# Banded attention: scores from float32r halves of q and k, three products in place of one fp32 product

## The chip, the cores and the metric

The kernel runs as one program on 1 core of one Trainium2 chip. The metric is the device time of that core in microseconds (us), from runs of the whole program. TensorE is called PE, its weight loads PEld, VectorE DVE, ScalarE ACT, GpSimd POOL and the SyncE queue SP. One execution was taken with the hardware profiler; its rows are what the texts below read.

## The reference, cut to what matters

The model is a trunk of two layers over 256 positions of width 2048. The first layer mixes by retention, the second by a sliding-window attention; each layer then has a SwiGLU block and a gated embedding. The change touches the attention mixer alone:

```python
proj = h @ w_in
q, k, v = jnp.split(proj, [SWA_Q_WIDTH, SWA_Q_WIDTH + SWA_KV_WIDTH], axis=-1)
q = (q * (HD ** -0.5)).reshape(B, NB, W, HKV, G, HD)      # 2 blocks of 128, 4 kv heads, 8 heads each, 64 wide
...
s = jnp.einsum('bqkgd,bskd->bkgqs', qb, kb).astype(jnp.float32) + alibi
s = jnp.where(valid, s, -jnp.inf)
m = jnp.maximum(jnp.max(s, axis=-1, keepdims=True), sink)
e = jnp.exp(s - m)
probs = e / (jnp.sum(e, axis=-1, keepdims=True) + jnp.exp(sink - m))
return jnp.einsum('bkgqs,bskd->bqkgd', probs.astype(vb.dtype), vb)
```

There are 32 query heads in 4 groups of 8; each group shares one k and one v. A query block of 128 sees its own block and the one before it, so the first block has 128 keys and the second 256.

## The kernel before, in words

All large products are made in float32r from two halves. A weight unit (128 x 2 x 512, 512 KB) is loaded on SP, ACT copies it to a float32r tile `hi` (L211), DVE subtracts to get `lo` (L212), and `multiply` issues, for each of 2 k-tiles and 2 row tiles, three products: high by high (L161), high by low (L162), low by high (L163). One unit is 12 products of 512 columns on PE; units are loaded 5 ahead and split 3 ahead.

The work between the large products is held in generators on the list `side`. After each unit, `step_side` runs every generator to its next `yield`. So the source gives an order in which small pieces of attention stand between units. The scheduler of the framework then lays out each engine's queue from that, with its own estimates, and may move small pieces past each other; each engine works through its queue in that fixed order and waits on semaphores of the others.

In the attention stage `kv_done` scales k and v; its `later` transposes k on PE into a PSUM tile `tr` (2 buffers, `transpose_pair`, L224) and copies it into `kT` with DVE (L436). For each of the 4 kv heads, `q_done` scales eight heads of q, and its `later` transposes them (8 transposes, two `tr` tiles) and copies one `tr` with DVE (L527) and the other with ACT (L525) into `qT`. Then come four calls of `scores(i)`, two heads each: 64 rows of the PE array hold one head (e = 0), the other 64 the second (e = 1). Per head there are two plain fp32 products (L460), of 128 columns for block 0 and of 256 for block 1, into two PSUM tiles `at` (2 buffers). DVE adds the bias (L470), takes the maximum (L479) and makes the exponents' offset `nm` (L488); ACT makes the exponentials with row sums (L493) and those of the sinks (L496); `normalise` adds (L500), inverts (L502) and scales (L506, four per call); `transpose_probs` transposes them on PE (L512) into `tr`, and DVE (L516) and ACT (L514) copy them into `pT`. The products with v are L544, and their result is split (L211, L212) into `oT`, which feeds the output projection.

The helper at the centre of the change is the split, which for an unscaled source is an ACT copy followed by a DVE subtraction that reads the ACT result:

```python
nc.scalar.activation(hi, src, AF.Copy)
nc.vector.tensor_tensor(lo, src, hi.bitcast(F32), op=ALU.subtract)
```

Of the kernel before, what the change touches and what calls it, by code (L numbers as in the profile page):

```python
# [11 lines left out]
F32 = mybir.dt.float32  # L12
F32R = mybir.dt.float32r
# [5 lines left out]
P = 128  # L19
D = 2048  # L20
S = 256
# [8 lines left out]
SH, SD, SKV = 32, 64, 4  # L30
# [57 lines left out]
def tile_trunk(ctx, tc, ins, out):  # L88
    nc = tc.nc
# [313 lines left out]
    def swa(norm, next_norm, w_in, w_out):  # L403
        ol = Lhs()
        st = {}
# [10 lines left out]

        def kv_done(acc):
            sp = stage.pool
            kT = st["kT"] = sp.tile([P, SKV, S], F32, name="kT")
            v = st["v"] = sp.tile([P, NT, SKV * SD], F32, name="vs")  # L420
            kd = sp.tile([P, NT, SKV, 2, SD], F32, name="kd")
            inv8 = st["inv8"] = sp.tile([P, NT], F32, name="inv8")
            nc.vector.tensor_scalar_mul(inv8, norm.inv, SD**-0.5)
            for t in range(NT):
                src = acc[t][:, 0 : SKV * SD].rearrange("p (j d) -> p j d", d=SD)
                for e in range(2):
                    nc.scalar.activation(kd[:, t, :, e, :], src, AF.Copy, scale=norm.inv[:, t : t + 1])
                nc.scalar.activation(
                    v[:, t, :], acc[t][:, SKV * SD : 2 * SKV * SD], AF.Copy, scale=norm.inv[:, t : t + 1]
                )  # L430

            def later():
                for i in range(2):
                    yield
                    tr = transpose_pair(blocks(lambda t: kd[:, t].rearrange("p j e d -> p (j e d)"), i))
                    nc.vector.tensor_copy(kT[:, 2 * i : 2 * i + 2, :], tr)  # L436

            return later()

        def q_done_of(j):  # L440
            def q_done(acc):
                sp, kT, v, rel = stage.pool, st["kT"], st["v"], st["rel"]
                q = sp.tile([P, NT, NW], F32, name="q")
                for t in range(NT):
                    nc.scalar.activation(q[:, t, :], acc[t], AF.Copy, scale=st["inv8"][:, t : t + 1])
                qT = sp.tile([P, 4, S], F32, name="qT")
                sc = sp.tile([P, GH, 3, P], F32, name="sc")
                pT = sp.tile([P, 3, 2, 4, P], F32, name="pT")

                def block(h, b):  # L450
                    blk = sc[:, h, 0:1, :] if b == 0 else sc[:, h, 1:3, :]
                    return blk.rearrange("p a b -> p (a b)")

                def scores(i):

                    ats = [ps_at.tile([P, 3 * P], F32, name="at") for _ in range(2)]
                    for b in range(2):
                        for e in range(2):
                            sl = slice(e * SD, (e + 1) * SD)
                            nc.tensor.matmul(  # L460
                                ats[e][:, 0:P] if b == 0 else ats[e][:, P : 3 * P],
                                qT[sl, i, b * P : (b + 1) * P],
                                kT[sl, j, 0 : (b + 1) * P],
                                start=True,
                                stop=True,
                            )
                    hs = slice(2 * i, 2 * i + 2)
                    for e in range(2):
                        h = 2 * i + e
                        nc.vector.scalar_tensor_tensor(  # L470
                            out=sc[:, h].rearrange("p a b -> p (a b)"),
                            in0=rel,
                            scalar=-(2.0 ** (-8.0 * (j * GH + h + 1.0) / SH)),
                            in1=ats[e],
                            op0=ALU.mult,
                            op1=ALU.add,
                        )
                    mx = small.tile([P, 2, 3], F32, name="mx")
                    nc.vector.reduce_max(mx, sc[:, hs], axis=AX.X)  # L479
                    sk = st["sink"][:, j * GH + 2 * i : j * GH + 2 * i + 2]  # L480
                    nc.vector.tensor_tensor(mx[:, :, 1], mx[:, :, 1], mx[:, :, 2], op=ALU.max)
                    mm = small.tile([P, 2, 2], F32, name="mm")
                    es = small.tile([P, 2, 2], F32, name="es")
                    for b in range(2):
                        nc.vector.tensor_tensor(mm[:, b, :], mx[:, :, b], sk, op=ALU.max)
                        nc.vector.tensor_tensor(es[:, b, :], sk, mm[:, b, :], op=ALU.subtract)
                    nm = small.tile([P, 2, 2], F32, name="nm")
                    nc.vector.tensor_scalar_mul(nm, mm, -1.0)  # L488
                    den = small.tile([P, 2, 2], F32, name="den")
                    for e in range(2):  # L490
                        for b in range(2):
                            blk = block(2 * i + e, b)
                            nc.scalar.activation(  # L493
                                blk, blk, AF.Exp, bias=nm[:, b, e : e + 1], accum_out=den[:, b, e : e + 1]
                            )
                    nc.scalar.activation(es, es, AF.Exp)  # L496
                    return den, es

                def normalise(i, den, es):
                    nc.vector.tensor_tensor(den, den, es, op=ALU.add)  # L500
                    rd = small.tile([P, 2, 2], F32, name="rd")
                    nc.vector.reciprocal(rd, den)  # L502
                    for e in range(2):
                        for b in range(2):
                            blk = block(2 * i + e, b)
                            nc.vector.tensor_scalar_mul(blk, blk, rd[:, b, e : e + 1])  # L506

                def transpose_probs(i):
                    for e in range(2):
                        tr = ps_tr.tile([P, 3, P], F32, name="tr")  # L510
                        for b in range(3):
                            nc.tensor.transpose(tr[:, b, :], sc[:, 2 * i + e, b, :], ident)  # L512
                        if e:
                            nc.scalar.copy(pT[:, :, e, i, :], tr)  # L514
                        else:
                            nc.vector.tensor_copy(pT[:, :, e, i, :], tr)  # L516

                def later():

                    yield  # L520
                    yield
                    for i in range(2):
                        tr = transpose_pair(blocks(lambda t: q[:, t, :], i))
                        if i:
                            nc.scalar.copy(qT[:, 2 * i : 2 * i + 2, :], tr)  # L525
                        else:
                            nc.vector.tensor_copy(qT[:, 2 * i : 2 * i + 2, :], tr)  # L527
                    for i in range(4):
                        yield
                        part = scores(i)  # L530
                        if i > 1:
                            transpose_probs(i - 2)
                        yield
                        normalise(i, *part)
                    yield
                    transpose_probs(2)
                    yield
                    transpose_probs(3)
                    yield
                    for b in range(2):  # L540
                        o = ps_at.tile([P, 4, P], F32, name="at")
                        for e in range(2):
                            for m in range(b + 1):
                                nc.tensor.matmul(  # L544
                                    o[e * SD : (e + 1) * SD, :, :],
                                    v[:, m, j * SD : (j + 1) * SD],
                                    pT[:, 0 if b == 0 else 1 + m, e, :, :],
                                    start=m == 0,
                                    stop=m == b,
                                )  # L550
                        ks, sl = slice(4 * j, 4 * j + 4), slice(b * P, (b + 1) * P)
                        split(ol.hi[:, ks, sl], ol.lo[:, ks, sl], o)
                    ol.ready.update(range(4 * j, 4 * j + 4))

                return later()

            return q_done
# [5 lines left out]
        n = KD // KU  # L563
# [303 lines left out]
```

## Time and profile before

| | us |
|---|---|
| median of 3 runs (2621.5 to 2621.99) | 2621.93 |
| the profiled execution, its own time | 2622.02 |
| its span, first to last instruction | 2619.9 |
| PE busy in the span | 2607.7 |
| DVE busy | 1814.4 |
| ACT busy | 1223.2 |

The attention's score products lie between about 1602 and 1722 us of the span. A matmul's own duration is longer than the distance to the next, since matmuls overlap in the array; what a stretch costs on PE is read from the distances between starts. In the timeline one plain fp32 product is two records, one float32r product is one; equal instructions that follow each other are merged into one row with their count.

### The profile page before, as it was taken

Reading aid. Unit: us, or ns where it says so; the run is one execution under the profiler, and the core shown is the slowest. Engines: PE = TensorE matmul, PEld = TensorE weight load, DVE = VectorE, ACT = ScalarE, POOL = GpSimd, SP = SyncE. Lnnn points to the kernel's source line nnn. Section 1 sums busy time; section 2 is a strip of 40 time slices with the busy share of each in tenths; the row PEclk is TensorE's granted clock in tenths of the full one; section 3 lists DMA queues with packets and bytes.
Section 4 is the critical chain, followed back from the end, with each engine's and each line's share of the span. In section 5 each row is a group of like instructions: output and inputs, shape, how many; then the busy total and the mean of one; then the engine's idle time right before and its main releaser. Section 6 shows DMA issues by size and latency. Waiting matters only on the chain.

```text
span 2619.9 us, 31288 instructions
## 1 busy us (share of the span) xinstructions
PE 2607.7 (100%) x11641; PEld 2144.0 (82%) x11641; DVE 1814.4 (69%) x2563; ACT 1223.2 (47%) x1531; POOL 15.1 (1%) x31
## 2 busy tenths in 40 slices
PE   9999999999999999999999999999999999999998
PEld 7888888888888888888888888777888888888887
DVE  7777777766666666666555786888757575755565
ACT  6444444444444444444444555555444444444444
POOL 0000000000000000000000000000000000000000
PEclk9999999999999999999999999999999999999999
DMA  8556555566666666666666665346665666666664
GB/s 288 187 186 188 184 188 179 185 186 191 196 194 198 189 199 189 197 191 195 193 194 193 191 196 169 123 144 199 190 198 189 198 189 198 190 196 193 193 209 144
DMA packets 139481, 497.79 MB, mean 190 GB/s; under 512 B 15808, under 2 KB 16960, under 8 KB 139200
## 3 DMA queue, kind: packets, MB, share of 16 engines
q1 hardware_dynamic: 139040, 495.73, 60.5%
q8 instruction: 91, 1.49, 0.2%
q14 instruction: 62, 0.51, 0.1%
q10 hardware_dynamic: 288, 0.07, 0.0%
HBM read 493.63 MB, written 2.10 MB: 189 GB/s over the span
## 4 chain that ended last, share of the span: by engine, by line
PE 94%; DVE 3%; DMA 1%; issue 1%; ACT 0%; POOL 0%; ACTq 0%; POOLq 0%; SPq 0%; DVEq 0%
PE acc L161 31%; PE acc L163 30%; PE acc L162 30%; DVE xt L236 1%; DVE lo L212 1%; PE at L460 1%; DMA x<-in_xT 1%; PE tr L512 0%; DMA xs<-in_x 0%; PE at L544 0%; PE at L329 0%; DVE xTl L215 0%; DMA pt<-in_pT 0%; PE at L356 0%; PE at L358 0%
## 5 line engine op out<-in xcount | busy, mean ns | idle before, releaser
L212 DVE TENSOR_TENSOR lo<-raw,hi 128x1024 fp32r<-128x1024 f32 (+1 forms) x929 | 1131.3, 1221 | 701.2 <-ACT hi L211 693.7
L211 ACT ACTIVATE hi<-raw 128x1024 fp32r<-128x1024 f32 (+1 forms) x929 | 980.8, 1058 | 1186.8 <-PE acc L163 1074.9
L161 PE MATMUL acc<-hi,xTh 128*128 128x512 f32 x2592 | 1009.5, 390 | 0.7 <-ACT hi L211 0.5
L163 PE MATMUL acc<-hi,xTl 128*128 128x512 f32 x2592 | 1008.1, 389 | 1.2 <-DVE xTl L215 1.2
L162 PE MATMUL acc<-lo,xTh 128*128 128x512 f32 x2592 | 1008.1, 389 | 0.0
L161 PEld LDWEIGHTS acc<-hi,xTh 128*128 128x128 f32 x2592 | 487.1, 188 | 104.4 <-issue 3.0
L163 PEld LDWEIGHTS acc<-hi,xTl 128*128 128x128 f32 x2592 | 487.0, 188 | 103.8 <-DVE xTl L215 2.1
L162 PEld LDWEIGHTS acc<-lo,xTh 128*128 128x128 f32 x2592 | 487.1, 188 | 100.9 <-DVE lo L212 0.8
L161 PE MATMUL acc<-hi,hTh 128*128 128x512 f32 x704 | 273.9, 389 | 0.0
L162 PE MATMUL acc<-lo,hTh 128*128 128x512 f32 x704 | 273.9, 389 | 0.0
L163 PE MATMUL acc<-hi,hTl 128*128 128x512 f32 x704 | 273.9, 389 | 0.0
L236 DVE STREAM_TRANSPOSE xt<-h 32x256 f32<-32x256 f32 x352 | 153.4, 436 | 6.8
L161 PEld LDWEIGHTS acc<-hi,hTh 128*128 128x128 f32 x704 | 132.2, 188 | 27.7
L162 PEld LDWEIGHTS acc<-lo,hTh 128*128 128x128 f32 x704 | 132.2, 188 | 27.4
L163 PEld LDWEIGHTS acc<-hi,hTl 128*128 128x128 f32 x704 | 132.2, 188 | 27.2
L236 DVE STREAM_TRANSPOSE xt<-xs 32x256 f32<-32x256 f32 x320 | 139.5, 436 | 6.0
L161 PE MATMUL acc<-hi,yTh 128*128 128x512 f32 x256 | 99.6, 389 | 0.0
L162 PE MATMUL acc<-lo,yTh 128*128 128x512 f32 x256 | 99.6, 389 | 0.0
L163 PE MATMUL acc<-hi,yTl 128*128 128x512 f32 x256 | 99.6, 389 | 0.0
L214 ACT ACTIVATE xTh<-xt,gains 128x256 fp32r<-128x256 f32 x80 | 35.7, 499 | 61.0 <-DVE xt L236 56.5
L236 DVE STREAM_TRANSPOSE xt<-qk 32x256 f32<-32x256 f32 x128 | 55.8, 436 | 9.8 <-ACT qk L321 7.8
L236 DVE STREAM_TRANSPOSE xt<-y 32x256 f32<-32x256 f32 x128 | 55.8, 436 | 2.5
(128 smaller groups left out, 1169.4 us busy)
## 6 DMA issues: line engine op xcount, KB each, us to landing
raw<-in_ffn_w_in SPq DMA_DIRECT2D x352, 512.0 KB, 4.2
raw<-in_ret_w_in SPq DMA_DIRECT2D x191, 512.0 KB, 3.7
raw<-in_ffn_w_out SPq DMA_DIRECT2D x176, 512.0 KB, 4.2
raw<-in_ret_w_out SPq DMA_DIRECT2D x64, 512.0 KB, 4.1
raw<-in_ple_w_gate SPq DMA_DIRECT2D x64, 512.0 KB, 4.1
raw<-in_swa_w_in SPq DMA_DIRECT2D x40, 512.0 KB, 3.6
raw<-in_swa_w_out SPq DMA_DIRECT2D x32, 512.0 KB, 3.7
raw<-in_ple_w_proj SPq DMA_DIRECT2D x8, 512.0 KB, 4.0
```

What stands on the lines that cost most here:

```text
L161: nc.tensor.matmul(ch.acc[n], xh, hi[:, j, cols], start=first, stop=False)
L162: nc.tensor.matmul(ch.acc[n], xh, lo[:, j, cols], start=False, stop=False)
L163: nc.tensor.matmul(ch.acc[n], xl, hi[:, j, cols], start=False, stop=last)
L211: nc.scalar.activation(hi, src, AF.Copy)
L212: nc.vector.tensor_tensor(lo, src, hi.bitcast(F32), op=ALU.subtract)
L214: nc.scalar.activation(hi, src, AF.Copy, scale=scale)
L236: nc.vector.transpose(dst[b * SQ : (b + 1) * SQ, :, :, a, :], src[a * SQ : (a + 1) * SQ, :, :, b, :])
L460: nc.tensor.matmul(ats[e][:, 0:P] if b == 0 else ats[e][:, P : 3 * P], qT[sl, i, b * P : (b + 1) * P], kT[sl, j, 0 : (b + 1) * P], start=True,
```

## The change

`kT` and `qT` become pairs of float32r tiles (kTh, kTl and qTh, qTl), filled by `split` in place of a single copy. The score product of one head and block becomes three float32r products that add up in PSUM: qTh by kTh, qTh by kTl, qTl by kTh. Line numbers behind the products move by one (L470 becomes L471, L512 becomes L513), and those behind the transposes of q by minus two (L544 becomes L542).

```diff
@@ kv_done @@
-            kT = st["kT"] = sp.tile([P, SKV, S], F32, name="kT")
+            kT = st["kT"] = [sp.tile([P, SKV, S], F32R, name=n) for n in ("kTh", "kTl")]
...
-                    nc.vector.tensor_copy(kT[:, 2 * i : 2 * i + 2, :], tr)
+                    split(*(k[:, 2 * i : 2 * i + 2, :] for k in kT), tr)
@@ q_done @@
-                qT = sp.tile([P, 4, S], F32, name="qT")
+                qT = [sp.tile([P, 4, S], F32R, name=n) for n in ("qTh", "qTl")]
...
                     for b in range(2):
-                        for e in range(2):
-                            sl = slice(e * SD, (e + 1) * SD)
-                            nc.tensor.matmul(
-                                ats[e][:, 0:P] if b == 0 else ats[e][:, P : 3 * P],
-                                qT[sl, i, b * P : (b + 1) * P],
-                                kT[sl, j, 0 : (b + 1) * P],
-                                start=True,
-                                stop=True,
-                            )
+                        for n, (x, y) in enumerate(((0, 0), (0, 1), (1, 0))):
+                            for e in range(2):
+                                sl = slice(e * SD, (e + 1) * SD)
+                                nc.tensor.matmul(
+                                    ats[e][:, 0:P] if b == 0 else ats[e][:, P : 3 * P],
+                                    qT[x][sl, i, b * P : (b + 1) * P],
+                                    kT[y][sl, j, 0 : (b + 1) * P],
+                                    start=n == 0,
+                                    stop=n == 2,
+                                )
...
                         tr = transpose_pair(blocks(lambda t: q[:, t, :], i))
-                        if i:
-                            nc.scalar.copy(qT[:, 2 * i : 2 * i + 2, :], tr)
-                        else:
-                            nc.vector.tensor_copy(qT[:, 2 * i : 2 * i + 2, :], tr)
+                        split(*(q_[:, 2 * i : 2 * i + 2, :] for q_ in qT), tr)
```

The change also alters the order that the scheduler lays out. Three places follow, each before and after. `tr` is the PSUM tile of transposes, `at` that of scores, `sc` the score tile in SBUF, `es`, `nm`, `den` and `rd` small tiles of the softmax.

PE's queue at the first scores of the second kv head, twelve large products behind the transposes of its q. Before:

```order
L163 MATMUL acc<-hi,xTl 128x512
L512 MATMUL tr<-ident,sc 128x128 x6
L460 MATMUL at<-kT,qT 128x128 x2
L460 MATMUL at<-kT,qT 128x256 x2
L161 MATMUL acc<-hi,xTh 128x512
```

The same place in the changed kernel:

```order
L163 MATMUL acc<-hi,xTl 128x512
L461 MATMUL at<-kTh,qTh 128x128 x2
L461 MATMUL at<-kTl,qTh 128x128 x2
L161 MATMUL acc<-hi,xTh 128x512
L162 MATMUL acc<-lo,xTh 128x512
L513 MATMUL tr<-ident,sc 128x128 x3
L461 MATMUL at<-kTh,qTl 128x128 x2
L513 MATMUL tr<-ident,sc 128x128 x3
L461 MATMUL at<-kTh,qTh 128x256 x2
L461 MATMUL at<-kTl,qTh 128x256 x2
L461 MATMUL at<-kTh,qTl 128x256 x2
```

The group of scores moved ahead of the transposes of the kv head before, and is cut into three stretches by two large products and two threes of transposes. The same is found at the third and the fourth kv head.

ACT's queue at the q tiles of the third kv head. Before:

```order
L211 ACTIVATE hi<-raw 128x1024
L525 COPY qT<-tr 128x512
L496 ACTIVATE es<-es 128x4
L493 ACTIVATE sc,den<-sc,nm 128x128
L493 ACTIVATE sc,den<-sc,nm 128x256
L493 ACTIVATE sc,den<-sc,nm 128x128
L493 ACTIVATE sc,den<-sc,nm 128x256
L211 ACTIVATE hi<-raw 128x1024
```

In the changed kernel:

```order
L211 ACTIVATE hi<-raw 128x1024
L494 ACTIVATE sc,den<-sc,nm 128x128
L494 ACTIVATE sc,den<-sc,nm 128x256
L494 ACTIVATE sc,den<-sc,nm 128x128
L494 ACTIVATE sc,den<-sc,nm 128x256
L497 ACTIVATE es<-es 128x4
L211 ACTIVATE qTh<-tr 128x512 x2
L211 ACTIVATE hi<-raw 128x1024
```

The copy out of `tr` stood ahead of the exponentials of the last group of the kv head before; the two halves stand behind them.

DVE's queue at the last group of scores of the fourth kv head. Before:

```order
L488 TENSOR_SCALAR nm<-mm 128x4
L470 SCALAR_TENSOR_TENSOR sc<-rel,at 128x384 x2
L516 COPY pT<-tr 128x3x128
L479 TENSOR_REDUCE mx<-sc 128x6
L500 TENSOR_TENSOR den<-den,es 128x4
```

In the changed kernel:

```order
L489 TENSOR_SCALAR nm<-mm 128x4
L501 TENSOR_TENSOR den<-den,es 128x4
L471 SCALAR_TENSOR_TENSOR sc<-rel,at 128x384
L503 RECIPROCAL rd<-den 128x4
L471 SCALAR_TENSOR_TENSOR sc<-rel,at 128x384
```

The reading of the new scores (L470, now L471) moved behind the sum `den` of the group before, which needs that group's exponentials from ACT. In these three engines nothing but the attention stage moved; SP's and POOL's queues are as before.

## Rows read from the trace of the kernel before

**Rows 1.** The page: busy us, share of the span and instructions of each engine.
```profile
PE 2607.7 (100%) x11641; PEld 2144.0 (82%) x11641; DVE 1814.4 (69%) x2563; ACT 1223.2 (47%) x1531; POOL 15.1 (1%) x31
```

**Rows 2.** The page's chain that ended last, by engine.
```profile
PE 94%; DVE 3%; DMA 1%; issue 1%; ACT 0%; POOL 0%; ACTq 0%; POOLq 0%; SPq 0%; DVEq 0%
```

**Rows 3.** Stretch of one kv head: PE, PEld, DVE, ACT, POOL busy; clock, DMA.
```profile
1649.00:1683.00 34.00, 34.00 (x179) 24.75 (x180) 27.68 (x78) 20.19 (x55) 0.00 (x0) 1.00 0.40 124
```

**Rows 4.** Timeline of PE, one whole group: start us, duration us, instruction.
```profile
1601.92 0.39 PE L163 MATMUL acc<-hi,xTl 128*128 128x512 f32 x1
1602.24 0.93 PE L460 MATMUL at<-kT,qT 64*128 64x128 f32 x8
1603.09 0.50 PE L161 MATMUL acc<-hi,xTh 128*128 128x512 f32 x1
1603.43 0.39 PE L162 MATMUL acc<-lo,xTh 128*128 128x512 f32 x1
```

**Rows 5.** Timeline of PE, a stretch of scores of one head alone.
```profile
1641.82 0.92 PE L460 MATMUL at<-kT,qT 64*128 64x128 f32 x4
1642.67 0.50 PE L163 MATMUL acc<-hi,xTl 128*128 128x512 f32 x1
```

**Rows 6.** Timeline of PE near the end: float32r products of 256 columns.
```profile
2609.00 0.28 PE L163 MATMUL at<-hi,xTl 128*128 128x256 f32 x1
2609.12 0.28 PE L161 MATMUL at<-hi,xTh 128*128 128x256 f32 x1
```

**Rows 7.** Timeline of PE between the q transposes and the next scores.
```profile
1660.44 1.06 PE L224 MATMUL tr<-ident,q 128*128 128x128 f32 x8
1661.25 0.47 PE L161 MATMUL acc<-hi,xTh 128*128 128x512 f32 x1
...
1664.08 0.82 PE L512 MATMUL tr<-ident,sc 128*128 128x128 f32 x6
1664.83 0.93 PE L460 MATMUL at<-kT,qT 64*128 64x128 f32 x8
```

**Rows 8.** Timeline of DVE in the same stretch.
```profile
1657.38 0.16 DVE L500 TENSOR_TENSOR den<-den,es 128x4 f32<-128x4 f32 x1 [0.90 <-ACT es L496]
...
1660.84 1.22 DVE L212 TENSOR_TENSOR lo<-raw,hi 128x1024 fp32r<-128x1024 f32 x1
1661.97 0.15 DVE L486 TENSOR_TENSOR es<-sink,mm 128x2 f32<-128x2 f32 x1
...
1662.11 0.68 DVE L527 COPY qT<-tr 128x512 f32<-128x512 f32 x1
1662.71 0.15 DVE L486 TENSOR_TENSOR es<-sink,mm 128x2 f32<-128x2 f32 x1
1662.78 0.16 DVE L488 TENSOR_SCALAR nm<-mm 128x4 f32<-128x4 f32 x1
```

**Rows 9.** Timeline of ACT in the same stretch.
```profile
1662.90 0.20 ACT L496 ACTIVATE es<-es 128x4 f32<-128x4 f32 x1 [0.69 <-DVE es L486]
1663.01 0.39 ACT L493 ACTIVATE sc<-sc,nm 128x128 f32<-128x128 f32 x1
...
1664.77 1.04 ACT L211 ACTIVATE hi<-raw 128x1024 fp32r<-128x1024 f32 x1
```

**Rows 10.** Groups by line and shape: the split of a 128x512 PSUM tile.
```profile
L212 DVE TENSOR_TENSOR oTl<-at,oTh 128x512 fp32r<-128x512 f32 x8 | 5.5, 686 | 0.7 <-ACT oTh L211 0.7
L211 ACT ACTIVATE oTh<-at 128x512 fp32r<-128x512 f32 x8 | 4.7, 593 | 3.4 <-PE at L544 3.4
```

**Rows 11.** Timelines of DVE and PE: the last group of the fourth kv head.
```profile
1721.70 1.02 DVE L470 SCALAR_TENSOR_TENSOR sc<-rel,at 128x384 f32<-128x384 f32 x2
...
1723.96 0.15 DVE L500 TENSOR_TENSOR den<-den,es 128x4 f32<-128x4 f32 x1
...
1730.16 1.01 DVE L506 TENSOR_SCALAR sc<-sc,rd 128x128 f32<-128x128 f32 x4
...
1731.18 0.82 PE L512 MATMUL tr<-ident,sc 128*128 128x128 f32 x6
```

## The prediction

> **What bounds the kernel now.** I read the page's busy times first, then the chain, then the stage. PE is busy 2607.7 us of a span of 2619.9, DVE 69% [rows 1], and the chain of waits lies on PE for 94% [rows 2]. In the stretch of one kv head PE is busy 34.00 of 34 us at a granted clock of 1.00, DVE 27.68 and ACT 20.19 [rows 3]. So whatever the change takes from or adds to PE's queue, in work or in waiting, moves the end one for one. DVE and ACT have time to spare on average, but not at every place, and each keeps a fixed queue: for this change I read the timelines of the three engines side by side, at the places where the order moved.
>
> The sum stands against the profiled execution's own 2622.02 us, span 2619.9 and 2.1 around it; the median of the runs, 2621.93, is the same within 0.1.
>
> **The score products on PE.** A whole group (two heads, plain fp32) starts at 1602.24 and the next large product at 1603.09, 0.85 us [rows 4]. Around it PE loses more: the product before it started 0.32 earlier where large products follow each other every 0.236 (12 in 2.83) [rows 7], so 0.09 going in, and the first large product behind it takes 0.34, 0.11 too much [rows 4]. A stretch costs 1.05 us. Each fp32 product is two records and the two heads run side by side, so there are four steps. Work in them is 0.85 less one uncovered load (0.11, as for the large product behind) and one emptying of the array (0.09): 0.65 us. The other 0.40 is entering and leaving the 64-row arrangement, a load and an emptying each way. That the two heads do share the time is seen where they don't: one head alone also takes 0.85 (1641.82 to 1642.67) [rows 5].
>
> The changed group has six steps, three of 128 columns and three of 256, each with its own load of 128 weight columns. No row shows a float32r product of 128 columns or one on 64 rows. From below: streaming alone, half and a quarter of the 0.213 that 512 columns take at the granted 2.4 GHz [rows 3], 0.107 and 0.053. From above: 128 columns as slow as the plain fp32 pair, 0.213. The nearest row is the float32r product of 256 columns with its own load, every 0.12 us [rows 6]; and eight 128-column transposes, which stream half as much, still take 0.81, 0.10 each [rows 7]. So the load is the floor, and I take 0.12 for every step: 6 x 0.12 = 0.72 per stretch.
>
> The Trainium skill, "TensorE: Matmul & The Clock Gate", section "Back-to-back issue gap", puts a lone warm product at N/2.4 + 2.5 ns, 56 ns for 128 columns; by that 18 stretches would work 18 x (3 x 0.056 + 3 x 0.109) = 8.9 us, an estimate, and this term would be a gain of 3. Its section "LDWEIGHTS (loading the stationary operand)" has 128 columns cost 107 ns whatever the rows; the 0.10 and 0.12 above side with the second.
>
> Count of stretches, from the order: 19 before (16 groups, 3 of them cut so that each head runs alone), 24 after: 11 whole groups, 3 cut in three pieces (the first group of the second to fourth kv head), 2 cut head by head in two, 9 + 4 + 11 = 24. Work: 19 x 0.65 = 12.35 before; after, 14 groups side by side and 2 head by head, 18 x 0.72 = 12.95. That is +0.6 us (from below 18 x 0.48, -3.7; from above 18 x 1.0, +5.65). Switching: 5 more x 0.40 = +2.0 us. The Trainium skill, "TensorEngine Tiling", section "Key Properties", says that a change of the tiling mode drains TensorE; the 0.40 us is what this trace shows of it, and it speaks against the change only because the new order cuts more.
>
> **The waits that the new order makes.** Here is the larger part. At the second to fourth kv head the scores now stand directly behind twelve large products, and the transposes of the old head, which gave 0.75 us of cover [rows 7], behind them. They need qTh from ACT; and ACT makes it behind the four exponentials of the last group, where before the copy stood ahead of them. In the trace, at the third kv head: PE is through its twelve products at 1664.08 and with the switch at 1664.17 [rows 7]. The exponentials start at 1663.01 and ACT is free at 1664.77 [rows 9]; they wait for nm at 1662.78, which closes a DVE chain that began with den at 1657.68, 5.40 us [rows 8]. In the new order this chain has no copy of qT (1662.11 to 1662.71, -0.60), but one more weight subtraction ahead of the score reading (1660.84 to 1661.97, +1.13) [rows 8]: exponentials 0.53 later, done at 1665.30, sinks +0.11 [rows 9], first half of qTh +0.59 [rows 10], 0.03 to PE: 1666.03. PE waits 1.9 us. So also at the fourth kv head. At the second the order holds no additional subtraction, and the wait is 1.9 - 1.13, 0.7. Together 4.5 us.
>
> Within each cut group a second wait follows: the transposes need a `tr` tile, which is free only when DVE has subtracted qTl; before, a plain copy freed it. DVE has den and rd (0.4) and four scalings (1.0) ahead of it [rows 11], then 0.69 [rows 10]. With the exponentials done 0.73 before the group starts, that frees `tr` 1.4 after its start; PE is there after 1.0 (two steps 0.24, load 0.11, out 0.2, two products 0.45), and loads uncovered after a wait, 0.1. Some 0.5 each: 1.5 us.
>
> Last group of the fourth kv head: the score reading started at 1721.70, and the scaled result came at 1731.17, with PE's transposes at 1731.18 [rows 11]; no slack. Now the reading stands behind den, which came at 1723.96 [rows 11], some 2.0 later with what lies between much the same. The large products around it don't change. I take 1.6 us, since DVE had 0.4 of a wait to give.
>
> What is queued behind each of these waits on PE is everything, as all later work is on the same queue, and nothing gives it back: PE has no idle time later.
>
> **What costs nothing.** For k the two DVE copies become two subtractions of the same 0.69, and ACT gains two copies of 0.59 [rows 10]; PE has a unit to do before either is read. For q, ACT makes eight of 0.59 for four, DVE eight of 0.69 for four, +2.7 us on DVE over the stage, which 6.3 idle us per kv head hide [rows 3]; uncovered it would be 2.7 us. Weights are split three units ahead, with no PE wait in this stage before. DMA is unaffected: its order is the same, and its share 0.40 [rows 3].
>
> **Sum:** 0.6 + 2.0 + 4.5 + 1.5 + 1.6 = 10.2 us on 2622.0: **2632.2 us**, 0.4% slower.
>
> **Rivals.** (1) The waits don't come: DVE reaches nm of the last group so early that ACT has qTh before PE has done its twelve products. It must gain 1.9 us on the 5.4 us chain, of which only waits for PE and ACT can go; for it speaks DVE's 19% of idle time [rows 3], against it that den starts when the exponentials end and nothing in the chain but 0.60 is taken out. Then 0.6 + 2.0 remain, 2624.6, which counts as no change; with streaming alone (-3.7) 2620.3. It decides from 1.9 us of DVE lead on. Chance 0.12; for a clear gain, 2616.8 or less, both would have to hold and the cuts be free besides, 0.02. (2) Narrow float32r products run as slowly as plain fp32: 0.213 per step of 128 columns. No row excludes it. Work +5.65 instead of +0.6; the longer groups let DVE and ACT come nearer, 0.3 per group, and the waits fall from 7.6 to about 5: 2622.0 + 5.65 + 2.0 + 5 = 2634.7. Chance 0.20. (3) The two heads' float32r products don't share the array: 14 x 0.72 = 10 more of work, waits down to 3, 2637.7. Against it, fp32 products on the same rows do share; 0.05. My forecast, six steps of 0.12 and the waits above, has the remaining 0.61, with its own range 2628 to 2636.
>
> A measurement of this kernel tells about 0.2%, 5.2 us, from no change. Slower than that: forecast, (2) and (3), 0.86; within it, rival (1), 0.12; faster 0.02. The range that leaves out most of (1) and the far end of (3) is 2626 to 2637.
>
> **What would show it.** In the changed profile: starts of L461 pairs about 0.12 apart (0.21 at 128 columns would be rival 2; twelve steps instead of six, rival 3); 24 stretches of L461; before the first of them at the second, third and fourth kv head an idle PE of some 0.7, 1.9 and 1.9 us released by ACT qTh; an idle L513 of about 0.4 released by DVE qTl; an idle L513 of 1 to 2 us near the stage's end; the large products after it as before, moved by about 10 us. A stage that ends less than 4 us late would prove the waits wrong; one that ends in time with the difference elsewhere, the whole account.

## The result and the profile after

The changed kernel takes 2638.13 us (median of 4 runs, 2636.26 to 2638.45) beside 2621.96 us of the kernel before (4 runs, 2621.5 to 2623.29): 1.0059 of its time, 95% interval 1.0047 to 1.0071. It is slower, as forecast, but by 16 us where 10 were forecast, and 1.1 us above the range. The profiled execution took 2638.45 us, its span 2636.3.

The page after, busy us and share of the span of each engine, and the chain by engine:

```profile
PE 2615.2 (99%) x11705; PEld 2150.8 (82%) x11705; DVE 1818.7 (69%) x2567; ACT 1226.9 (47%) x1537; POOL 15.1 (1%) x31
...
PE 97%; DVE 2%; issue 1%; ACT 0%; DMA 0%; SPq 0%; ACTq 0%; POOLq 0%; POOL 0%; DVEq 0%
```

PE is busy 7.5 us more than in [rows 1] while the span grew by 16.4, so about 9 us are idle time of PE. These are PE's waits in the attention stage (1620 to 1756 us; total, times, longest); the same view of the kernel before is empty:

```profile
PE at L461 <- ACT qTh L211: 4.2, 3, 1.6
PE tr L513 <- DVE qTl L212: 1.4, 3, 0.5
PE tr L513 <- DVE sc L507: 1.3, 1, 1.3
```

The three kinds of wait are those of the prediction, in number and nearly in size: 4.2 for 4.5, 1.4 for 1.5, 1.3 for 1.6. What the products themselves cost is seen on PE where nothing waits; the rows answer to [rows 4]:

```profile
1604.09 0.39 PE L163 MATMUL acc<-hi,xTl 128*128 128x512 f32 x1
1604.41 0.33 PE L461 MATMUL at<-kTh,qTh 64*128 64x128 f32 x2
1604.57 0.28 PE L461 MATMUL at<-kTl,qTh 64*128 64x128 f32 x2
1604.68 0.27 PE L461 MATMUL at<-kTh,qTl 64*128 64x128 f32 x2
1604.80 0.33 PE L461 MATMUL at<-kTh,qTh 64*128 64x256 f32 x2
1604.97 0.28 PE L461 MATMUL at<-kTl,qTh 64*128 64x256 f32 x2
1605.09 0.28 PE L461 MATMUL at<-kTh,qTl 64*128 64x256 f32 x2
1605.30 0.50 PE L161 MATMUL acc<-hi,xTh 128*128 128x512 f32 x1
```

Six steps, 0.11 to 0.12 us apart and 0.16 to 0.17 behind the first product of each width, the same for 128 and for 256 columns, the two heads in one row (x2): 0.89 us from the first score to the next large product, against 0.85. A whole stretch between large products, with its way in and out, is 1.08 us for 1.05. That term of the forecast stands.

Now the third kv head, in PE's timeline (rows in brackets tell idle time and its releaser):

```profile
1670.58 0.33 PE L461 MATMUL at<-kTh,qTh 64*128 64x128 f32 x2 [1.62 <-ACT qTh L211]
...
1672.15 0.90 PE L513 MATMUL tr<-ident,sc 128*128 128x128 f32 x3 [0.47 <-DVE qTl L212]
...
1674.21 0.58 PE L461 MATMUL at<-kTh,qTh 64*128 64x256 f32 x2
1674.59 0.42 PE L461 MATMUL at<-kTl,qTh 64*128 64x256 f32 x2
...
1675.75 0.63 PE L161 MATMUL acc<-hi,xTh 128*128 128x512 f32 x1
1676.17 0.63 PE L162 MATMUL acc<-lo,xTh 128*128 128x512 f32 x1
```

The two waits are there, and behind them something the prediction had no word for: the large products start 0.43 us apart, not 0.23, and the scores of 256 columns 0.22, not 0.11. Busy time of PE, PEld, DVE, ACT and POOL in stretches, then the granted clock, for the first to the fourth boundary (2nd, 3rd, 4th kv head and the tail):

```profile
1635.00:1640.00 5.00, 4.64 (x29) 3.61 (x30) 2.59 (x4) 0.85 (x3) 0.00 (x0) 1.00 0.43 128
1671.00:1675.00 4.00, 3.53 (x18) 2.24 (x16) 3.38 (x7) 1.43 (x3) 0.00 (x0) 0.60 0.33 112
1675.00:1680.00 5.00, 5.00 (x21) 3.96 (x18) 0.30 (x1) 0.58 (x1) 0.00 (x0) 0.63 0.32 105
1711.00:1715.00 4.00, 3.53 (x18) 2.33 (x17) 3.02 (x5) 1.07 (x2) 0.00 (x0) 0.72 0.23 83
1746.00:1751.00 5.00, 3.65 (x19) 2.82 (x18) 4.08 (x9) 3.21 (x7) 0.00 (x0) 1.00 0.40 131
```

Behind the waits at the 3rd and 4th kv heads the granted clock was on its lower level (1.2 GHz) for some microseconds; behind those at the 2nd and at the tail it stayed at 1.00. A third piece lies far from the change, in the first 14 us:

```profile
10.80 0.73 PE L161 MATMUL acc<-hi,xTh 128*128 128x512 f32 x2 [1.91 <-ACT hi L211]
12.06 0.50 PE L162 MATMUL acc<-lo,xTh 128*128 128x512 f32 x1 [0.52 <-DVE lo L212]
...
13.20 0.63 PE L161 MATMUL acc<-hi,xTh 128*128 128x512 f32 x1
```

PE waited 1.9 us for an early weight unit and then ran its products at half clock (0.43 apart) until about 16 us. The kernel before ran its very first products at half clock instead.

The starts of the same large product in two traces, later kernel minus kernel before, put sizes to these pieces. From here on this difference is called the offset, in us:

| at the large product that starts, in the kernel before, at | 47 | 1603 | 1629 | 1654 (2nd kv head) | 1687 (3rd) | 1723 (4th) | 1738 (tail) | end |
|---|---|---|---|---|---|---|---|---|
| changed kernel | 2.15 | 2.20 | 2.29 | 4.68 | 10.64 | 14.80 | 16.57 | 16.43 |
| the same kernel again | 0.94 | 0.95 | 1.03 | 5.00 | 11.18 | 13.86 | 15.64 | 15.48 |

### The profile page after: what moved, and what is told of

It reads as the page before. It is cut to its first block, busy times and chain, and to the rows that moved or that the text cites. A ratio compares the mean times of both kernels' runs of the same rounds, so it can differ in the third digit from the quotient of the medians.

```text
span 2636.3 us, 31417 instructions
## 1 busy us (share of the span) xinstructions
PE 2615.2 (99%) x11705; PEld 2150.8 (82%) x11705; DVE 1818.7 (69%) x2567; ACT 1226.9 (47%) x1537; POOL 15.1 (1%) x31
## 4 chain that ended last, share of the span: by engine, by line
PE 97%; DVE 2%; issue 1%; ACT 0%; DMA 0%; SPq 0%; ACTq 0%; POOLq 0%; POOL 0%; DVEq 0%
PE acc L163 31%; PE acc L161 31%; PE acc L162 31%; PE at L461 1%; DVE lo L212 1%; DVE xt L236 1%; PE tr L513 1%; PE at L542 0%; DMA raw<-in_ret_w_in 0%; PE at L329 0%; ACT sc L494 0%; PE at L357 0%; PE at L358 0%; PE at L356 0%; PE tr L224 0%
```

## The experiments

Two theories stood: Q, that the new order makes PE wait and that the waits let the clock fall; and P, that three products with their mode switches cost the time wherever they stand. Times are medians, ratios are to the kernel before on the same chip.

**1. The arithmetic whole, the order as before.**

```diff
+    behind = []   # the next weight's lo is issued after q's lo
...
+            with ExitStack() as es:
+                for ins in behind:
+                    es.enter_context(tc.issue_after(ins.ins))
+                split(hi[:, part, :], lo[:, part, :], raw[:, part, :])
...
-                        split(*(q_[:, 2 * i : 2 * i + 2, :] for q_ in qT), tr)
+                        with tc.high_priority():
+                            behind.append(split(*(q_[:, 2 * i : 2 * i + 2, :] for q_ in qT), tr))
...
+                        if j == SKV - 1 and i == 3:
+                            with tc.issue_after(part[2].ins):   # behind the reading of scores(3)
+                                normalise(2, *old)
```

> The changed kernel's arithmetic whole, in about the queue order of the kernel before: the halves of q are made ahead of the score group, the next weight's low half behind q's low half on VectorE, and the last normalise behind the scores that stand ahead of it. Theory Q (the order makes 7.7 us of waits, the waits let the clock halve, about 4.5 us, and the work itself is some 2 us): 2624 to 2626 us, by whether the 2.2 us lost in the first 14 us are there again; no PE gap over 0.6 us at the first scores of the 2nd to 4th kv heads, granted clock 1.00 there. Rival P (three products, their mode switches and the extra elements cost the time wherever they stand): 2634 to 2638 us with the waits gone or moved.

Measured: 2622.24 us (11 runs), ratio 1.0, 0.9991 to 1.0009. PE had no wait in the stage; all scores were in 18 stretches. The offset was 0.60 at 47 us and 0.72 at the end. The two stretches that hold the three boundaries and the tail:

```profile
1630.00:1680.00 50.00, 50.00 (x275) 36.70 (x274) 41.77 (x109) 28.98 (x79) 0.00 (x0) 1.00 0.41 137
1680.00:1750.00 70.00, 70.00 (x375) 53.88 (x376) 57.16 (x145) 41.41 (x102) 0.00 (x0) 1.00 0.40 128
```

PE is busy throughout at a clock of 1.00, with every product and every half of the changed kernel. P falls: the whole 16 us is order and what follows from it. The time lies under Q's range as well, since Q had set some 2 us for the work; with 18 stretches for 19, each 0.03 dearer, it costs nothing that the runs can show.

**2. The three products without halves.**

Against the kernel before, whose copies into kT and qT stay:

```diff
-            kT = st["kT"] = sp.tile([P, SKV, S], F32, name="kT")
+            kT = st["kT"] = sp.tile([P, SKV, S], F32R, name="kT")
...
-                qT = sp.tile([P, 4, S], F32, name="qT")
+                qT = sp.tile([P, 4, S], F32R, name="qT")
...
+                        for n in range(3):
...
+                                    start=n == 0,
+                                    stop=n == 2,
```

> Three float32r products per score but no halves: q and k are copied once each to float32r, so all three products are of the rounded values (the low halves are left out). Rival P: nearly all of the 16 us stays, 2634 us or more. Theory Q: no second step behind the exponentials, so the waits at the first scores and their clock loss go; left are about 2 us of work and switches, the tail's wait of 1.5 us and some tenths at the transposes: 2625 to 2629 us.

Measured: 2624.77 us, ratio 1.0008, 0.9999 to 1.0017, 0.2 us under Q's range. Two waits are left, and the offset grew by 2.4 us from 47 us on, 0.8 at the 2nd kv head and 1.7 at the tail, where they lie; without them hardly anything would be left:

```profile
PE tr L513 <- DVE sc L507: 1.3, 1, 1.3
PE tr L513 <- ACT qT L526: 0.6, 1, 0.6
```

The tail's wait is here without any low half. It comes with the three products, not with the subtractions: experiment 3, which has those, is without it.

**3. The halves with one plain product.**

```diff
-                        for n, (x, y) in enumerate(((0, 0), (0, 1), (1, 0))):
...
+                                qT[1][sl, i, b * P : (b + 1) * P].bitcast(F32),
+                                kT[0][sl, j, 0 : (b + 1) * P].bitcast(F32),
```

> The halves alone: q and k are split as in the changed kernel, but each score is one plain fp32 product, of q's low and k's high half (the other two products are left out, so the scores are not those of the reference). Theory Q: the extra steps delay the next transposes, but the score group is not cut as in the changed kernel, so the long waits come only in part: 2624 to 2630 us. Rival P: the split is cheap, 2621 to 2624 us.

Measured: 2625.6 us, ratio 1.0011, 1.0002 to 1.002, inside Q's range; the waits were

```profile
PE tr L512 <- DVE qTl L212: 1.5, 3, 0.5
```

The halves alone give the three waits for the `tr` tile, 0.5 each, and no wait at the scores; the offset grew by 0.9 at each of the three, 0.4 beside the wait. Neither part alone gives the 4.2 us at L461, and neither lost clock in the stage: only both together made the scheduler put the score group ahead of all six transposes and cut it (here it stands between the two threes, and whole).

**4. Work in the place of the wait.**

```diff
+                    for _ in range((0, 8, 14, 14)[j] if i == 0 else 0):
+                        nc.tensor.matmul(
+                            ats[0][:, P : 3 * P], xT[0][:, 0, 0:P], xT[0][:, 0, 0 : 2 * P], start=True, stop=True
+                        )
```

> The changed kernel, with 8, 14 and 14 products of 256 columns that nobody reads put on TensorE ahead of the first scores of the 2nd, 3rd and 4th kv heads, so that TensorE works while q's halves are made. Theory Q (the idle time is what lets the clock fall): granted clock 1.00 after the three places, and 3 to 5 us less than the changed kernel though work was added: 2633 to 2636 us. Rival (the clock falls by the half-array products themselves, or by chance): clock down to a half as in the changed kernel, 2638 to 2641 us.

Measured: 2635.78 us (2633.84 to 2636.97), ratio 1.005, 1.0037 to 1.0062. The added products did cover the wait for qTh, but PE then waited for the `tr` tile (4.7 us, longest 1.8): the total, the waits at the 2nd and 3rd kv heads, and the stretches behind the 2nd, 3rd and 4th.

```profile
PE tr L517 <- DVE qTl L212: 4.7, 3, 1.8
...
1634.81 0.55 PE L517 MATMUL tr<-ident,sc 128*128 128x128 f32 x3 [1.25 <-DVE qTl L212]
...
1673.74 0.55 PE L517 MATMUL tr<-ident,sc 128*128 128x128 f32 x3 [1.76 <-DVE qTl L212]
...
1635.00:1640.00 5.00, 5.00 (x24) 3.80 (x24) 2.04 (x3) 0.48 (x1) 0.00 (x0) 0.66 0.36 120
1674.00:1679.00 5.00, 5.00 (x36) 4.11 (x35) 1.97 (x3) 0.65 (x2) 0.00 (x0) 1.00 0.35 120
1711.00:1716.00 5.00, 4.83 (x33) 3.96 (x34) 2.41 (x4) 0.48 (x1) 0.00 (x0) 1.00 0.37 125
```

Half a confirmation at most. At the 3rd and 4th kv heads the clock stayed at 1.00; but there the added products also changed the order, and the score group stood behind the transposes in one stretch (20 stretches in all for 24). At the 2nd, where the changed kernel's clock had not fallen, it fell, behind a wait of 1.3 us. So the length of one wait doesn't decide it (the wait at the 3rd, 1.8 us, was the longer). The time lies in Q's range, in part by luck: it is 2.4 us under the changed kernel's and not 3 to 5, with the clock lost at one place and new waits at all three. This run can't tell the theory of idle time from chance; the next two can.

**5. The changed kernel again**, unaltered.

> The changed kernel again, not altered. In its first profile 2.2 us were lost in the first 14 us and the clock fell to a half behind the waits at the 3rd and 4th kv heads, not behind the 2nd's. If the start has to do with the change: 2.1 us of PE gap near 10 us again and 2636 to 2638.5 us. If the start and the place of the clock drops are chance: another gap there, drops at other ones of the three places, and single times that spread over 2 to 5 us. The waits themselves (1.0, 1.7, 1.7 and 1.5 us and three of 0.55 us) the same in either case.

Measured: 2636.7 us (2636.14 to 2637.95), ratio 1.0056, 1.0042 to 1.007. The waits were the same to 0.1 us, and the clock fell elsewhere: behind the 2nd and the 3rd kv head, not behind the 4th. First the wait at the 4th kv head, in the first profile of the changed kernel and in this one; then this one's stretches behind the 2nd, 3rd and 4th.

```profile
1710.22 0.33 PE L461 MATMUL at<-kTh,qTh 64*128 64x128 f32 x2 [1.59 <-ACT qTh L211]
...
1710.76 0.33 PE L461 MATMUL at<-kTh,qTh 64*128 64x128 f32 x2 [1.59 <-ACT qTh L211]
...
1635.00:1640.00 5.00, 5.00 (x21) 3.83 (x21) 1.38 (x2) 0.48 (x1) 0.00 (x0) 0.66 0.36 107
1675.00:1680.00 5.00, 5.00 (x15) 3.79 (x14) 0.00 (x0) 0.15 (x1) 0.00 (x0) 0.52 0.32 105
1711.00:1715.00 4.00, 3.52 (x24) 2.35 (x23) 3.58 (x7) 1.62 (x3) 0.00 (x0) 1.00 0.32 112
```

The two rows of the table above now give the price of the fall, boundary by boundary: at the 2nd kv head 2.39 us without and 3.97 with it, so 1.6; at the 4th 2.68 without and 4.16 with it, 1.5; at the 3rd, where it fell both times and stayed low about twice as long, 6.0 and 6.2 against some 2.7 for equal waits, so 3.3 and 3.5. That is 4.8 us in the first profile and 5.1 in the second. At the start only 0.94 us was lost this time (the first wait there was 0.77 us instead of 1.91, and the clock did not fall). The other profiles lie between -0.4 and +1.6 there, over kernels that differ in the attention stage alone; the start is chance, not the change. The two profiles may come from two chips, and that this has a part in where the clock falls is not excluded.

**6. A wait alone, in the kernel before.**

```diff
                             nc.vector.tensor_copy(qT[:, 2 * i : 2 * i + 2, :], tr)
+                            for _ in range((0, 5, 6, 7)[j]):
+                                nc.gpsimd.tensor_copy(qT[:, 0:2, :], qT[:, 0:2, :])
```

> The kernel before with one thing added: GpSimd writes the first two q heads of the 2nd, 3rd and 4th kv head over with themselves 5, 6 and 7 times ahead of their first scores, so that TensorE has to wait there although its products stay plain fp32 and the score groups whole. One such copy is estimated at 0.5 to 1 us (GpSimd's 128x512 bf16 fill takes 0.52 us), which makes waits of some 1 to 4 us. Theory idle (a wait alone lets the clock fall): granted clock under 1.00 behind the longer waits, and 1.5 us or more per place lost beyond the gap. Rival (it also takes the small products and second waits of the cut score group): clock 1.00 throughout, and the time grows by the gaps alone.

Measured: 2636.87 us (2634.03 to 2637.25), ratio 1.0054, 1.0041 to 1.0066. The waits, and the clock behind them:

```profile
PE at L460 <- POOL qT L529: 8.3, 3, 3.6
...
1635.12 0.93 PE L460 MATMUL at<-kT,qT 64*128 64x128 f32 x8 [2.17 <-POOL qT L529]
...
1673.40 1.05 PE L460 MATMUL at<-kT,qT 64*128 64x128 f32 x8 [2.50 <-POOL qT L529]
...
1712.75 1.65 PE L460 MATMUL at<-kT,qT 64*128 64x128 f32 x8 [3.63 <-POOL qT L529]
...
1635.00:1640.00 5.00, 4.88 (x19) 3.72 (x20) 1.54 (x3) 0.00 (x0) 0.07 (x1) 0.66 0.34 116
1673.00:1678.00 5.00, 4.60 (x18) 3.34 (x19) 1.42 (x1) 0.00 (x0) 0.35 (x1) 0.66 0.33 105
1712.00:1719.00 7.00, 6.25 (x23) 4.77 (x24) 0.86 (x3) 1.23 (x2) 0.69 (x1) 0.54 0.23 75
```

Plain fp32 products, whole score groups, one single wait at each place: gaps of 2.6, 2.9 and 4.0 us between starts, 0.32 of each being the way into the scores; the profile counts 2.2, 2.5 and 3.6 of them as idle. The clock fell behind all three, and the offset grew by 3.8, 4.1 and 6.3 us, 1.5, 1.5 and 2.6 more than the gaps explain. The rival falls: idle time of PE is enough, and neither float32r nor a cut score group nor a second wait is needed. The small products of the scores stood behind the waits here too; but in the first 14 us of the changed kernel the clock fell among large products alone. A wait of 2.2 us costs 1.5 us more behind it.

**7. The first step of experiment 1 by itself.**

```diff
-                        split(*(q_[:, 2 * i : 2 * i + 2, :] for q_ in qT), tr)
+                        with tc.high_priority():
+                            split(*(q_[:, 2 * i : 2 * i + 2, :] for q_ in qT), tr)
```

> The changed kernel with the q halves alone put ahead of the score group (one priority); the next weight's low half may still stand ahead of q's low half on VectorE and the tail is as it was. Theory Q: the waits at the first scores go and the group is no longer cut in pieces; left are waits of 0.3 to 1.1 us at the transposes of the three boundaries and 1.5 us at the tail: 2626 to 2630 us, clock 1.00 there. Rival P (the products themselves): 2634 us or more.

Measured: 2627.3 us (11 runs), ratio 1.0019, 1.001 to 1.0028, in Q's range.

```profile
PE tr L513 <- DVE qTl L212: 1.9, 3, 0.9
PE tr L513 <- DVE sc L507: 1.4, 1, 1.4
```

The waits at L461 are gone, the score groups whole, the clock 1.00 from 1630 to 1750 us; PE waits 3.3 us in all, and the offset grew by 4.9 us from 47 us on (1.43 to 6.37), 1.6 more than the waits. One priority in one place takes back 9.4 of the 14.5 us that the changed kernel loses on the same chip (experiment 5); the two further steps of experiment 1 take the rest.

**8 to 10. Fewer stretches.** The first experiment's 18 stretches suggested that the price is the stretch, not the product in it. In the kernel before, one more yield keeps the layer's products from cutting the last score group of a kv head:

```diff
                     transpose_probs(3)
                     yield
+                    yield               # 8: for all kv heads
+                    if j < 2:           # 9 (and 10, on top of experiment 1): for the first two
+                        yield
```

> The kernel before (plain fp32 products) with one more yield ahead of the value products, so that the last score group of a kv head isn't cut in two by the layer's products. If each stretch of small products costs its switch of about 0.4 us, three or four stretches less make it 1 to 2 us faster: 2620.5 to 2621.5 us. If the switch isn't what a stretch costs: 2622 to 2623.5 us.

> As the yield before, but only for the first two kv heads: the extra yield saved 1.07 us at each of two boundaries and lost 0.85 us at the last kv head, where it cut another score group. Theory (each merged score group saves a stretch of small products): 2.1 us less than the kernel before, 2619.8 to 2620.5 us. If those offsets were particular to one profile: 2621 to 2622.5 us.

> The kernel with float32r halves in about the order of before (the first experiment), with the same yield for the first two kv heads, so that these last score groups stay whole too. Theory Q (the products themselves cost about nothing, a stretch costs by being one): 1 to 2 us less than the first experiment, 2620 to 2621.5 us, though 0.2 to 0.4 us may be left as waits at two transposes. Rival P (three products are dearer than two fp32 passes by 0.03 us a group and more): 2622 us or more.

| | us | ratio and interval | stretches |
|---|---|---|---|
| 8 | 2620.49 | 0.9994, 0.9986 to 1.0003 | 18 |
| 9 | 2620.16 | 0.9993, 0.9984 to 1.0002 | 17 |
| 10, float32r | 2621.49 | 0.9996, 0.9988 to 1.0005 | 16 |

In the profiles each merged group saves 1.07 us: in experiment 9 the offset goes from +0.42 to -0.65 and to -1.72 over the first two boundaries. That is a whole stretch, since two heads that run apart take as long each as both together [rows 5]. The medians of 8 and 9 lie 1.7 and 2.0 us under the kernel before, but their intervals reach past 1, so a gain over it is likely and not shown. All three come out within the ranges of their theories or at the edge, experiment 8 in part by luck: it has one stretch less, not three or four (two groups merged, and one cut in three at the last kv head), and a merged stretch gives 1.07 us, not 0.4. With float32r and all groups whole the time is 0.7 us under the kernel before, again inside the interval, and PE still waited 0.7 us for `tr` tiles (at L229 of that kernel). It is 1.3 us over experiment 9, the plain fp32 kernel in about the same order.

## Why the prediction was right and wrong

- **PE sets the end one for one**: right. The waits and the slower products of the stage all appear in the end's offset, 16.57 at the tail and 16.43 at the end.
- **Six steps of 0.12, +0.6 of work**: right. Steps are 0.11 to 0.17 apart; a stretch costs 0.03 more than before, where 0.07 was forecast. The rivals of slow narrow products (0.21 per step) and of heads that don't share the array (twelve steps) are refuted by the same rows.
- **24 stretches for 19, 0.40 each**: the count is right. The changed kernel's group at the 2nd kv head cost 2.39 us with 1.4 us of waits in it (0.96 and 0.47), so 0.9 for the two more pieces and for what follows each wait, beside 0.8 forecast. The two are not told apart: experiment 3 lost 0.4 us beside each wait with every score group as before. What a cut costs by itself is not shown.
- **The waits, 4.5, 1.5 and 1.6**: right in cause and releaser, 4.2, 1.4 and 1.3 us. At the scores 0.96, 1.62 and 1.59 stand for 0.7, 1.9 and 1.9. On ACT the chain was as forecast: the exponentials, the sinks and then both halves of q,

```profile
1668.08 0.40 ACT L494 ACTIVATE sc<-sc,nm 128x128 f32<-128x128 f32 x1 [1.64 <-DVE nm L489]
...
1669.85 0.19 ACT L497 ACTIVATE es<-es 128x4 f32<-128x4 f32 x1
1669.95 1.05 ACT L211 ACTIVATE qTh<-tr 128x512 fp32r<-128x512 f32 x2
```

  behind nm, which closes this chain on DVE:

```profile
1661.56 0.16 DVE L501 TENSOR_TENSOR den<-den,es 128x4 f32<-128x4 f32 x1 [2.03 <-ACT es L497]
...
1662.90 1.22 DVE L212 TENSOR_TENSOR lo<-raw,hi 128x1024 fp32r<-128x1024 f32 x1
...
1666.29 1.22 DVE L212 TENSOR_TENSOR lo<-raw,hi 128x1024 fp32r<-128x1024 f32 x1
...
1667.88 0.16 DVE L489 TENSOR_SCALAR nm<-mm 128x4 f32<-128x4 f32 x1
```

  From den to nm it is 6.3 us, 0.9 more than the 5.4 of [rows 8] (where den starts at 1657.38, not the 1657.68 of the prediction's text); 0.53 more was forecast. The second weight subtraction is in it as the order had shown. The wait was shorter than forecast all the same: den came only 4.2 us later than before, where the large products came 4.7 later. Two errors of 0.4 and 0.5 us cancel here; to that extent the agreement is luck.
- **"The large products after it as before", at "a granted clock of 1.00"**: here it failed. The forecast took the clock of [rows 3] as given, though that row is of a stretch in which PE never stops. The change puts stops there, and the clock falls behind two of the three kv heads, not the same two each time: 4.8 us of the first profile, 5.1 of the second, set at nothing in the sum without a reason. With it the forecast would have been 2637. The second set of runs of the same program, 2636.7, lies inside the range of 2626 to 2637, whose upper end was set for the rivals; the term was missing in either case.
- **The profiled execution as the base**: some 2 us of the first profile lie in the kernel's first 14 us, ahead of anything that was changed. The kernel before, too, spreads from 2621.4 to 2625.4 over its runs.

Sum of the profile: 2.2 at the start, 6.9 of waits, 4.8 of clock, and 2.5 left for the extra pieces and loads: 16.4. The forecast had 7.6, 0, and 2.6 for the last three. The waits are within 10%, and the miss is the term that it left out. The 2.5 is a remainder and no measured price of the cuts: experiment 7, without any group cut anew, lost 1.6 us beside its waits. That it comes out near 2.6 may be luck.

The Trainium skill, "TensorE: Matmul & The Clock Gate", section "What's actually happening", says that the chip's watch over TensorE runs free of the kernel, so that the same program meets it in another phase each time. The runs agree: equal waits of 1.59 and 0.47 us at the 4th kv head were followed by half clock in one profile and by full clock in the other. Where in its phase each wait fell is not worked out here.

## What to carry to other kernels

When a change makes a bounding TensorE wait, price the wait twice: for itself, and for the products behind it, which may start at half clock. Here waits of 1 to 2 us cost nothing, 1.5 or some 3.4 us on top, by chance, and waits of 2.2 us and more cost 1.5 us or more on top in all three cases. Before judging new arithmetic by its time, look where the scheduler put what feeds it: three products instead of one cost about 1 us or less in 2622 here, and one priority in the source took back most of the loss.

## What the runs showed of the hardware

- A float32r product of 128 columns on 64 rows of the array steps in 0.11 us as one of 256 columns does, with its own load, and two of them on the two halves of the rows share the step.
- PE idle for 1.3 us among small products (experiment 4, at the 2nd kv head) can be enough for the lower clock, and idle for 1.8 us (the same run, 3rd kv head) can leave it at 1.00.
- GpSimd copies 128 x 512 fp32 in SBUF in 0.84 us (18 copies), where VectorE took 0.68 us out of PSUM [rows 8]; the spans of GpSimd are rough.
